# A two-layer attention and state-space trunk: where the norm operations, a table's zeroing, the scaling of u and the layer boundary stand in the order

## The chip, the cores and the metric

The kernel runs on one core of one Trainium2 chip. The metric is the time of one execution on the device in microseconds (us); of several runs the median counts. The engines of the core work side by side, each through its own queue of instructions: TensorE (PE) multiplies, VectorE (DVE) and ScalarE (ACT) do the elementwise work, GpSimd (POOL) and SyncE (SP) are used for a few fills and for issuing DMAs. An instruction that needs another engine's result waits for it at the head of its queue, and everything behind it waits too.

## The reference, cut to what matters

The input is 256 positions of 2048 numbers in float32, and there are two layers. Each layer normalises its input, projects it with one matrix into six parts, runs two branches on them and adds their normalised output projection:

```
h = rmsnorm(x, pre_norm_g[l])
proj = h @ w_in[l]
q, k, v, z_att, u, z_ssm = split(proj)
o_att = diff_attention(q, k, v, lam, rel_bias)
o_att = rmsnorm(o_att, subln_g[l]) * (1.0 - lam_init) * silu(z_att)
y = s5_ssm(u, ...)              # a scan over the positions: 64 groups, 64 complex states
g_val, g_gate = split(gelu(y) @ w_glu[l])
o_ssm = g_val * sigmoid(g_gate) * silu(z_ssm)
mix = concat(o_att, o_ssm) @ w_out[l]
x = x + rmsnorm(mix, post_norm_g[l])
```

## The kernel before

**Weights.** All weights of both layers are streamed once, as 288 half chunks of 512 KB, 144 a layer, in the order u (first four tiles together, "U4", then tiles 4 to 7), q, k, v and z_att, z_ssm ("zs"), glu, out. Each comes by a DMA of SyncE into one of five buffers `raw`. ScalarE copies it to `hi`, a shortened form (fp32r) that TensorE multiplies faster, and VectorE computes `lo` = raw - hi. The activations are split in the same way into `ht` (`hthi` and `htlo`), `mx` or `ghi`/`glo`. TensorE multiplies hi by both halves and lo by the high half, 24 matmuls of 256 columns, or 12 of 512, for a half chunk. hi and lo have three buffers each and are made two half chunks ahead.

**One loop** over the half chunks (line 1224) writes the program. For each it emits the DMA of a later one, `hooks` (which starts generators at given steps s of the layer), `emit_hi` and `emit_lo` of the half chunk two ahead, and `main`, the matmuls. `run_first` and `run_second` advance the generators by one step between those: `prep_gen` (tables `cm`, `z`, `wi`, `gc` of the state-space branch), `rstd_gen` (the norm factor of the layer's input: squares, a chain of norm operations, `psr`, which spreads it over the partitions, and `rbc`, its copy), `s_gen` (`pss`, input of the scan), `scan_ops`, `y_gen` (`psy`, `psz`, gelu, `psg`), attention, and `evac`, which takes the finished sums out of PSUM (`ac` and `acu` are such sums).

**VectorE's fillers.** Two queues hold VectorE work that may go anywhere. `weave` holds long lists (parameters, z, scan), `urgent` holds norm chains: `newton_ops` computes 1/sqrt by two Newton steps (`nwy`, `nwh`; `a` and `scal` are input and result for the attention norm, `nv` and `rs` for one row half at a layer's end, `rst` for a layer's input). Both are emitted by `fill`, half of them before and half behind each lo; the room is `bal`, the planner's estimate of TensorE's time less VectorE's load, with `SPARE` taken off each step and 2880 ns for a step of u, q and k (line 1283). With a norm chain waiting the room is `UB` = 1500 ns, whatever the balance, and norm and weave operations take turns.

**The layer boundary** (lines 1229 to 1265). The last half chunks of the first layer are held back for the second row half, so that row half 0 can be normalised (`rowend(0)`, `add_ops`: `xt`) while TensorE still multiplies for row half 1. Then come one bank of transposes `psw` for the next layer's `wi`, `warm(W3)` dummy matmuls, `rowend(1)`, and `build`, the transposes `psx` of the new `xt` into `ht`. Without ready transposes TensorE can't begin the layer.

**The end.** `rowend(1)`, then `late_mg`: the multiplication of the last 512 columns of `mg` by the norm's weights, on GpSimd; then three pieces of `xt`, each stored by a DMA (TPS).

Of the kernel before, what the change touches and what calls it, by code (L numbers as in the profile page):

```python
# [10 lines left out]
F32 = mybir.dt.float32  # L11
# [28 lines left out]
W3 = 4  # L40
WB = 1
# [7 lines left out]
TPS = ([(0, 1024), (1024, 1024)], [(0, 512), (512, 768), (1280, 768)])  # L49
WY = 2  # L50
UB = 1500
# [35 lines left out]
def hybrid_trunk(ctx: ExitStack, tc, x, rel_bias, post_norm_g, xt_in, wst, vecs, poles, lams, bc, onehot, out):  # L87
# [118 lines left out]
    def fill(budget, force=False):  # L206
        while (budget > 0 and weave) or (urgent and (force or budget > 0)):
            if urgent:
                try:
                    budget -= next(urgent[0])  # L210
                except StopIteration:
                    urgent.popleft()
            if not weave or budget <= 0:
                continue
            try:
                budget -= next(weave[0])
            except StopIteration:
                weave.popleft()
# [19 lines left out]
    def emit_lo(hs, budget, halves=False, parts=(0, 1)):  # L238
        if hs >= 2 * NCH:
            return  # L240
        src, (hi, lo) = raw[hs], split[hs]
        if lo is None:
            lo = late[hs] if hs in late else sp.tile([128, 1024], F32R, tag="lo", name="lo")
        hf = hi.bitcast(F32)
        if (weave and budget > 0) or urgent:
            budget = UB if urgent else budget
            fill(budget / 2)
            tt(lo, src, hf, ALU.subtract)
            fill(budget / 2)
        elif halves:  # L250
            for p in parts:
                c = slice(512 * p, 512 * p + 512)
                tt(lo[:, c], src[:, c], hf[:, c], ALU.subtract)
        else:
            tt(lo, src, hf, ALU.subtract)
        split[hs] = (hi, lo)
        if parts[-1]:
            raw.pop(hs)

    def newton_ops(o, v, n, i=0):  # L260
# [3 lines left out]
        yield ts(y.bitcast(I32), v.bitcast(I32), -0.5, float(0x5F380000), ALU.mult, ALU.add)  # L264
        yield mul(h, y, y)
# [204 lines left out]
    def prep_gen(l, slots):  # L470
# [55 lines left out]
        for b0 in range(0, 8, nb):  # L526
# [11 lines left out]
            for b, ps in zip(range(b0, b0 + nb), pss):  # L538
                psv = ps.rearrange("p (h a g q) -> p h a g q", h=2, a=2, g=2)
                wv = wi[b // 4].rearrange("p (b h r a q) -> p b h r a q", b=4, h=2, r=2, a=2)[:, b % 4]  # L540
                for r in range(2):
                    for g in range(2):
                        act(wv[64 * g:64 * g + 64, :, r], psv[64 * r:64 * r + 64, :, :, g ^ r], AF.Copy)
# [63 lines left out]
    def build(l, m):  # L607
# [7 lines left out]
        for t in range(2):  # L615
            for i in range(2):
                k = 2 * m + i
                tpose(pss[i][:, 256 * i + 128 * t:256 * i + 128 * t + 128], xt[t][:, 128 * k:128 * k + 128], ident)
        for i in range(2):
# [7 lines left out]
    def rstd_gen(l):  # L627
# [43 lines left out]
        if l == 0:  # L671
            yield
# [46 lines left out]
    def s_gen(l):  # L719
# [6 lines left out]
        for b0 in range(0, 8, 2):  # L726
            if b0 == 4:
                while not (S["u2"] and f"wi{l}" in S):
                    yield
                yield  # L730
# [3 lines left out]
            for b in (b0, b0 + 1):  # L734
                wi = S[f"wi{l}" if b >= 4 else f"wa{l}"][b // 4]
                for h in range(2):
                    for a in range(2):
                        for r, g in ((0, 0), (1, 1), (1, 0), (0, 1)):
                            rows, o = slice(64 * g, 64 * g + 64), 64 * (g ^ r)
                            q, c = 2 * h + r, 256 * a + 64 * (2 * (b - b0) + h)  # L740
                            mm4(pss[r][o:o + 64, c:c + 64], wi[rows, b % 4, 2 * q + a], U[rows, 8 * q + b], True, True)
# [208 lines left out]
    def evac(l, seg, b, ac):  # L950
# [6 lines left out]
        if seg in ("U4", "u"):  # L957
            yield from until(f"rbc{l}")
            for j, a in enumerate(ac):
# [3 lines left out]
                mul(o, cut(a[:, 0:256]), cut(rbc))  # L963
        elif seg in ("q", "k"):
# [53 lines left out]
    def main(hs, only=None, part=None):  # L1018
# [3 lines left out]
        if seg == "U4":  # L1022
# [20 lines left out]
            else:  # L1043
                for kk in range(2) if part is None else (part,):
                    for pr in (None,) if part != 0 else range(3):
                        for j in range(4):
                            one(kk, j, pr)
# [79 lines left out]
    def hooks(l, s):  # L1127
# [20 lines left out]
        if s == 96 and l + 1 < DEPTH:  # L1148
# [38 lines left out]
    SPARE = (150.0, 200.0, 300.0)  # L1187
    LOT = 1225.0
    with tc.manual_schedule():
# [34 lines left out]
        for hs in range(2 * NCH):  # L1224
# [4 lines left out]
            if s == 0:  # L1229
# [13 lines left out]
                if l:  # L1243
# [3 lines left out]
                    warm(W3)  # L1247
                    rowend(1)
                    for _ in add_ops(l - 1, 1, [(0, 256), (256, 256)], False):
                        pass  # L1250
# [44 lines left out]
        for t in range(2):  # L1295
# [4 lines left out]
            late_mg(G, (t,))  # L1300
            for _ in add_ops(DEPTH - 1, t, TPS[t], True):
                pass
# [71 lines left out]
```

## Time and profile before

| | us |
|---|---|
| median of 3 runs | 923.97 (923.2 to 924.18) |
| the profiled execution | 924.31 |
| its span, first to last instruction | 922.5 |
| TensorE busy | 901.3 (98%) |
| VectorE busy | 674.2 (73%) |
| ScalarE busy | 487.1 (53%) |
| GpSimd busy | 13.7 (1%) |
| granted TensorE clock, mean | 0.99 |

The rows name an operation as out<-in, with the line of the kernel in front; where a helper emits it, the line is that of the helper (L139 a matmul, L123 a transpose, L142 an elementwise operation of two tensors, L149 one with two operations, L160 an activation). The bracket behind a row is the idle time of the engine just before it, and what ended that. Ends of matmuls are modelled, so durations of neighbours overlap; their starts tell more.

### The profile page before, as it was taken

The page shows a single profiled execution, that of the slowest core. Times are in us where ns is not written, and L with a number is a line of the kernel's source. Part 1 is how long each engine was busy: PE and PEld are TensorE (multiplying, and loading weights), DVE is VectorE, ACT ScalarE, POOL GpSimd, SP SyncE. Part 2 cuts the span into 40 slices and gives each one's busy share as a digit, 9 for nine tenths or more (in the row PEclk, how much of TensorE's full clock was granted, in tenths as well). Part 3 has the DMA queues.
Part 4 walks back from the last instruction along what each step waited for, and adds up shares of the span by engine and source line. Part 5 has one row for each costly group of instructions (what it writes and reads, how often), then busy time and mean ns, then how long its engine had stood idle before and what let it go on. Part 6 is the DMA issues. An engine that isn't in the chain of part 4 may idle for free.

```text
span 922.5 us, 16345 instructions
## 1 busy us (share of the span) xinstructions
PE 901.3 (98%) x6344; PEld 775.3 (84%) x6344; DVE 674.2 (73%) x1202; ACT 487.1 (53%) x878; POOL 13.7 (1%) x19
## 2 busy tenths in 40 slices
PE   9989999999999899999999999999999999999995
PEld 8989999888778688888889888887888888888884
DVE  5978894998975757898677549888966465665564
ACT  6623357465465576444469453445565665644451
POOL 2000000000000000000000000000000000000001
PEclk9999999999999999999999999999999999999998
DMA  8767566755452467567646765865545346665862
GB/s 326 233 190 233 182 218 170 224 176 166 138 183 94 136 224 233 172 226 242 211 152 188 247 209 130 267 198 168 178 137 182 116 138 205 203 208 165 293 181 92
DMA packets 65069, 176.11 MB, mean 191 GB/s; under 512 B 17574, under 2 KB 24512, under 8 KB 64096
## 3 DMA queue, kind: packets, MB, share of 16 engines
q1 hardware_dynamic: 64704, 174.89, 59.9%
q8 instruction: 50, 0.82, 0.4%
q14 instruction: 27, 0.22, 0.1%
q0 software_dynamic: 144, 0.15, 0.1%
q10 hardware_dynamic: 144, 0.03, 0.0%
HBM read 167.42 MB, written 7.88 MB: 190 GB/s over the span
## 4 chain that ended last, share of the span: by engine, by line
PE 86%; DVE 4%; ACT 2%; issue 1%; DVEq 0%; ACTq 0%
PE ac L139 78%; PE lga L139 1%; DVE lo L142 1%; PE psy L139 1%; PE po L139 1%; ACT wi L160 1%; PE pss L139 1%; DVE sct L142 1%; PE acu L139 1%; ACT hi L160 1%; PE pwt L123 1%; PE pst L139 0%; PE psm L123 0%; PE psf L123 0%; DVE nwh L142 0%
## 5 line engine op out<-in xcount | busy, mean ns | idle before, releaser
L160 ACT ACTIVATE hi<-raw 128x1024 fp32r<-128x1024 f32 (+1 forms) x282 | 298.1, 1057 | 358.8 <-PE ac L139 307.7
L142 DVE TENSOR_TENSOR lo<-raw,hi 128x1024 fp32r<-128x1024 f32 (+1 forms) x282 | 343.0, 1218 | 116.5 <-ACT hi L160 113.5
L139 PE MATMUL ac<-ht,hi 128*128 128x256 f32 (+1 forms) x1104 | 257.6, 319 | 3.7 <-DVE u L142 2.5
L139 PE MATMUL ac<-hi,ht 128*128 128x512 f32 x768 | 251.1, 398 | 0.0
L139 PEld LDWEIGHTS ac<-ht,hi 128*128 128x128 f32 x1104 | 184.3, 193 | 18.9 <-issue 2.9
L139 PE MATMUL ac<-ht,lo 128*128 128x256 f32 x704 | 199.3, 284 | 0.4 <-DVE lo L142 0.4
L139 PEld LDWEIGHTS ac<-hi,ht 128*128 128x128 f32 x768 | 144.9, 189 | 31.9
L139 PE MATMUL ac<-lo,ht 128*128 128x512 f32 x384 | 150.8, 393 | 2.1 <-DVE lo L142 2.0
L139 PE MATMUL ac<-hi,mx 128*128 128x512 f32 x456 | 141.8, 390 | 0.0
L139 PEld LDWEIGHTS ac<-ht,lo 128*128 128x128 f32 x704 | 135.2, 192 | 0.9 <-DVE lo L142 0.9
L139 PEld LDWEIGHTS ac<-hi,mx 128*128 128x128 f32 x456 | 85.6, 188 | 17.7
L139 PE MATMUL ac<-lo,mx 128*128 128x512 f32 x228 | 88.7, 389 | 0.0
L139 PEld LDWEIGHTS ac<-lo,ht 128*128 128x128 f32 x384 | 72.6, 189 | 17.5 <-DVE lo L142 3.7
L139 PE MATMUL ac<-hi,ghi 128*128 128x512 f32 x128 | 51.6, 403 | 0.0
L139 PEld LDWEIGHTS ac<-lo,mx 128*128 128x128 f32 x228 | 42.8, 188 | 8.9
L139 PE MATMUL ac<-hi,glo 128*128 128x512 f32 x128 | 50.2, 392 | 0.0
L139 PE MATMUL ac<-lo,ghi 128*128 128x512 f32 x128 | 49.9, 390 | 0.0
L149 DVE SCALAR_TENSOR_TENSOR y<-y 128x512 f32<-128x512 f32 x16 | 11.1, 692 | 28.2 <-ACT y L160 28.0
L160 ACT ACTIVATE att<-att,mx 128x128 f32<-128x128 f32 x64 | 28.4, 446 | 5.4 <-DVE mx L871 5.1
L139 PEld LDWEIGHTS ac<-hi,glo 128*128 128x128 f32 x128 | 24.0, 188 | 5.2
L139 PEld LDWEIGHTS ac<-lo,ghi 128*128 128x128 f32 x128 | 24.1, 188 | 4.6
L139 PEld LDWEIGHTS ac<-hi,ghi 128*128 128x128 f32 x128 | 24.0, 188 | 4.5
(202 smaller groups left out, 964.2 us busy)
## 6 DMA issues: line engine op xcount, KB each, us to landing
raw<-in_wst_dram SPq DMA_DIRECT2D x287, 512.0 KB, 4.0
U<-uds SPq DMA_DIRECT2D x48, 64.0 KB, 3.4
bt<-in_bc_dram SPq DMA_DIRECT2D x4, 512.0 KB, 6.4
uds<-u SPq DMA_DIRECT2D x4, 512.0 KB, 6.0
pg<-in_post_norm_g_dram SPq DMA_DIRECT2D x2, 1024.0 KB, 6.9
xt<-in_x_dram SPq DMA_DIRECT2D x2, 1024.0 KB, 7.4
xt<-xsave SPq DMA_DIRECT2D x2, 1024.0 KB, 6.2
tabs<-tab SPq DMA_DIRECT2D x1, 1536.0 KB, 8.3
```

What stands on the lines that cost most here:

```text
L123: P.transpose(o, i, idn)
L139: P.matmul(o, lhsT=l, rhs=r, start=start, stop=stop, skip_group_check=True)
L142: V.tensor_tensor(o, a, b, op=op)
L149: V.scalar_tensor_tensor(out=o, in0=a, scalar=s, in1=b, op0=op0, op1=op1)
L160: A.activation(out=o, in_=i, func=f, **kw)
```

## The change

Nine edits. (1) `fill` gives norm operations their own 330 ns before each half of the fill and whatever the balance, and weave operations only what the balance allows; UB goes. (2) `newton_ops` for one column (a row half at a layer's end) has seven operations where there were nine. (3) In layer 0 `rstd_gen` emits psr a step earlier, and `evac` of U4 scales its four banks before the three acu. (4) `prep_gen` for the next layer, with its zeroing of cm on GpSimd, its loads bt and its copies, starts at step 102 and not 96, and SPARE for the second part of layer 0 is 100. (5) wi is copied in three pieces a bank and not four. (6) The scan of layer 0 starts one half chunk earlier. (7) At the boundary two banks psw stand ahead of psx, and the dummy matmuls (six, each in two passes) stand behind the first psx. (8) In the first weights the matmuls are ordered hthi, lo, htlo. (9) At the end the multiplication of mg is VectorE's for the second row half, behind the second of three pieces 768, 768, 512.

```diff
-W3 = 4
-WB = 1
+W3 = 0
+WB = 2
+W5 = 6
-TPS = ([(0, 1024), (1024, 1024)], [(0, 512), (512, 768), (1280, 768)])
+TPS = ([(0, 1024), (1024, 1024)], [(0, 768), (768, 768), (1536, 512)])
-UB = 1500
...
-    def fill(budget, force=False):
-        while (budget > 0 and weave) or (urgent and (force or budget > 0)):
-            if urgent:
-                try:
-                    budget -= next(urgent[0])
-                except StopIteration:
-                    urgent.popleft()
-            if not weave or budget <= 0:
-                continue
+    def fill(budget):
+        left = 330.0
+        while urgent and left > 0:
+            try:
+                n = next(urgent[0])
+                left -= n
+                budget -= n
+            except StopIteration:
+                urgent.popleft()
+        while budget > 0 and weave:
...
-            budget = UB if urgent else budget
...
+        if n == 1:
+            w = st.tile([128, n], F32, tag=f"nww{i}", name="nww")
+            yield ts(w, v, 9.0 / 64.0, None, ALU.mult)
+            yield stt(h, y, y, v, ALU.mult, ALU.mult)
+            yield stt(h, h, -10.0 / 3.0, h, ALU.add, ALU.mult)
+            yield stt(y, h, 5.0, y, ALU.add, ALU.mult)
+            yield stt(h, y, y, w, ALU.mult, ALU.mult)
+            yield stt(o, h, -3.0, y, ALU.add, ALU.mult)
+            return
...
-                for r in range(2):
-                    for g in range(2):
-                        act(wv[64 * g:64 * g + 64, :, r], psv[64 * r:64 * r + 64, :, :, g ^ r], AF.Copy)
+                act(wv[:, :, 0], psv[:, :, :, 0], AF.Copy)
+                for g in range(2):
+                    act(wv[64 * g:64 * g + 64, :, 1], psv[64 - 64 * g:128 - 64 * g, :, :, 1], AF.Copy)
...
+            if not m and not t:
+                warm(W5)
...
-        if l == 0:
-            yield
         yield 1
         ps = side("psr")
...
-                yield
+                if l:
+                    yield
...
+            if l == 0 and seg == "u":
+                yield from until("u4")
...
+            if seg == "U4":
+                S["u4"] = True
...
-                for kk in range(2) if part is None else (part,):
-                    for pr in (None,) if part != 0 else range(3):
-                        for j in range(4):
-                            one(kk, j, pr)
+                ks = range(2) if part is None else (part,)
+                if l == 0 and b == 0 or part == 0:
+                    todo = [(kk, pr) for pr in ((0, 2, 1) if part is None else range(3)) for kk in ks]
+                else:
+                    todo = [(kk, None) for kk in ks]
+                for kk, pr in todo:
+                    for j in range(4):
+                        one(kk, j, pr)
...
-        if s == 96 and l + 1 < DEPTH:
+        if s == 102 and l + 1 < DEPTH:
...
-    SPARE = (150.0, 200.0, 300.0)
+    SPARE = (150.0, 100.0, 300.0)
...
-                    warm(W3)
+                    if W3:
+                        warm(W3)
                     rowend(1)
+                    for _ in range(2):
+                        advance(S["prep"])
...
-            late_mg(G, (t,))
-            for _ in add_ops(DEPTH - 1, t, TPS[t], True):
-                pass
+            if not t:
+                late_mg(G, (t,))
+            for n, _ in enumerate(add_ops(DEPTH - 1, t, TPS[t], True)):
+                if t and n == 1:
+                    late_mg(V, (t,))
```

What it moves is seen in the order of the instructions on an engine, at three places.

VectorE where u is scaled, in layer 0 (`pt` is a step of the parameter list, `ac_170` to `ac_173` are U4's four banks), before:

```order
L142 TENSOR_TENSOR lo<-raw,hi 128x1024
L149 SCALAR_TENSOR_TENSOR pt<-pt 128x64 x3
L154 TENSOR_SCALAR pt<-pt 128x64
L142 TENSOR_TENSOR u<-acu,rbc 128x16x4x4 x3
L142 TENSOR_TENSOR u<-ac_170,rbc 128x16x4x4
L142 TENSOR_TENSOR u<-ac_171,rbc 128x16x4x4
L142 TENSOR_TENSOR u<-ac_172,rbc 128x16x4x4
L142 TENSOR_TENSOR u<-ac_173,rbc 128x16x4x4
L142 TENSOR_TENSOR lo<-raw,hi 128x1024
```

and now:

```order
L142 TENSOR_TENSOR lo<-raw,hi 128x1024
L154 TENSOR_SCALAR pt<-pt 128x64
L149 SCALAR_TENSOR_TENSOR pt<-pt 128x64 x3
L142 TENSOR_TENSOR u<-ac_170,rbc 128x16x4x4
L142 TENSOR_TENSOR u<-ac_171,rbc 128x16x4x4
L142 TENSOR_TENSOR u<-ac_172,rbc 128x16x4x4
L142 TENSOR_TENSOR u<-ac_173,rbc 128x16x4x4
L142 TENSOR_TENSOR lo<-raw,hi 128x1024
L142 TENSOR_TENSOR u<-acu,rbc 128x16x4x4 x3
```

The four banks of U4 now stand ahead of lo and of the three acu.

VectorE at the second attention norm chain of layer 0 (`a`, `nwy`, `nwh`, `scal` are the chain; `zs` and `glo` are the gate of the state-space branch and a half of its activations; `y` is gelu's), before:

```order
L154 TENSOR_SCALAR a_3633<-a_3633 128x8
L156 TENSOR_SCALAR nwy<-a_3633 128x8
L142 TENSOR_TENSOR nwh<-nwy 128x8
L142 TENSOR_TENSOR lo<-raw,hi 128x1024
L142 TENSOR_TENSOR nwh<-nwh,a_3633 128x8
L149 SCALAR_TENSOR_TENSOR nwh<-nwh 128x8
L154 TENSOR_SCALAR a_3633<-a_3633 128x8
L149 SCALAR_TENSOR_TENSOR nwy<-nwh,nwy 128x8
L142 TENSOR_TENSOR nwh<-nwy 128x8
L149 SCALAR_TENSOR_TENSOR zs<-th,ac_3208 128x512
L149 SCALAR_TENSOR_TENSOR zs<-th,ac_3209 128x512
L142 TENSOR_TENSOR glo<-psg,ghi 128x16x16 x2
```

and now:

```order
L154 TENSOR_SCALAR a_3625<-a_3625 128x8
L142 TENSOR_TENSOR lo<-raw,hi 128x1024
L156 TENSOR_SCALAR nwy<-a_3625 128x8
L142 TENSOR_TENSOR nwh<-nwy 128x8
L142 TENSOR_TENSOR nwh<-nwh,a_3625 128x8
L149 SCALAR_TENSOR_TENSOR zs<-th,ac_3200 128x512
L149 SCALAR_TENSOR_TENSOR zs<-th,ac_3201 128x512
L142 TENSOR_TENSOR glo<-psg,ghi 128x16x16 x2
L149 SCALAR_TENSOR_TENSOR y<-y 128x512
L149 SCALAR_TENSOR_TENSOR nwh<-nwh 128x8
L154 TENSOR_SCALAR a_3625<-a_3625 128x8
L149 SCALAR_TENSOR_TENSOR nwy<-nwh,nwy 128x8
```

Behind the lo stands the chain's nwy and not its second nwh, and the next operation with one tensor input, `a`, stands behind y and not ahead of zs.

TensorE at the boundary of the layers (`ac_4872` and `ac_4864` are the sum of row half 1, `psw` transposes for wi, `psx` transposes of the new xt), before:

```order
L139 MATMUL ac_4872<-hi,mx 128x512
L123 MATMUL psw<-ident,z_4306 128x128 x4
L139 MATMUL warm<-ones 128x128 x4
L123 MATMUL psx<-ident,xt_4553 128x128 x2
L123 MATMUL psx<-ident,xt_4554 128x128 x2
L123 MATMUL psx<-ident,xt_4553 128x128 x2
L123 MATMUL psx<-ident,xt_4554 128x128 x2
L139 MATMUL ac_5093<-ht,hi 128x256 x2
```

and now:

```order
L139 MATMUL ac_4864<-hi,mx 128x512
L123 MATMUL psw<-ident,z_4298 128x128 x8
L123 MATMUL psx<-ident,xt_4545 128x128 x2
L139 MATMUL warm<-ones 128x128 x6
L123 MATMUL psx<-ident,xt_4546 128x128 x2
L123 MATMUL psx<-ident,xt_4545 128x128 x2
L123 MATMUL psx<-ident,xt_4546 128x128 x2
L139 MATMUL ac_5092<-ht,hi 128x256 x2
```

The dummy matmuls moved behind the first psx, and eight psw stand where four stood.

## Rows read from the trace of the kernel before

**Rows 1.** The page: busy time of each engine, and the granted TensorE clock by slice.

```profile
PE 901.3 (98%) x6344; PEld 775.3 (84%) x6344; DVE 674.2 (73%) x1202; ACT 487.1 (53%) x878; POOL 13.7 (1%) x19
...
PEclk9999999999999999999999999999999999999998
```

**Rows 2.** Waits of TensorE: engine, tile, line <- releaser: us in total, times, longest.

```profile
PE ac L139 <- DVE u L142: 2.5, 1, 2.5
PE ac L139 <- DVE lo L142: 2.4, 4, 0.9
PE psg L123 <- DVE nwh L142: 2.2, 1, 2.2
PE psx L123 <- DVE xt L149: 1.5, 1, 1.5
...
PE ac L139 <- DVE ht L149: 0.9, 1, 0.9
PE pss L139 <- ACT wi L160: 0.3, 1, 0.3
```

**Rows 3.** Stretches: length, busy us (count) by engine, granted clock, DMA share, GB/s.

```profile
50.00:60.00 10.00, 7.49 (x49) 7.12 (x48) 5.98 (x15) 2.39 (x3) 0.00 (x0) 0.83 0.43 139
470.00:480.00 10.00, 9.77 (x66) 9.34 (x67) 6.78 (x15) 7.15 (x17) 0.00 (x0) 0.83 0.55 171
228.00:255.00 27.00, 25.74 (x118) 20.07 (x117) 26.42 (x46) 11.13 (x19) 0.00 (x0) 1.00 0.48 139
```

**Rows 4.** Timeline of TensorE and VectorE at u: start, duration, engine, line, operation, [idle <-releaser].

```profile
50.73 0.59 PE L139 MATMUL psr<-dg,ones 128*128 128x256 f32 x2
53.84 0.47 PE L139 MATMUL ac<-ht,hi 128*128 128x256 f32 x2 [2.51 <-DVE u L142]
...
51.78 1.48 DVE L142 TENSOR_TENSOR u<-acu,rbc 128x256 f32<-128x256 f32 x3 [1.02 <-ACT rbc L160]
53.11 1.98 DVE L142 TENSOR_TENSOR u<-ac,rbc 128x256 f32<-128x256 f32 x4
```

**Rows 5.** Timeline of VectorE at the start of layer 0's scan.

```profile
161.17 1.23 DVE L142 TENSOR_TENSOR sct<-H,a4s 128x1024 f32<-128x1024 f32 x1 [2.02 <-ACT H L160]
```

**Rows 6.** Timeline of VectorE, GpSimd and TensorE at the second norm chain, layer 0.

```profile
306.60 1.22 DVE L142 TENSOR_TENSOR lo<-raw,hi 128x1024 fp32r<-128x1024 f32 x1
...
308.02 1.85 DVE L154 TENSOR_SCALAR a<-a 128x8 f32<-128x8 f32 x1
...
310.01 1.28 DVE L149 SCALAR_TENSOR_TENSOR zs<-th,ac 128x512 f32<-128x512 f32 x2
...
312.19 0.68 DVE L149 SCALAR_TENSOR_TENSOR y<-y 128x512 f32<-128x512 f32 x1
...
313.47 1.22 DVE L142 TENSOR_TENSOR lo<-raw,hi 128x1024 fp32r<-128x1024 f32 x1
...
308.04 1.81 POOL L475 MEMSET cm<- 128x2048 f32 x1 [143.38 <-PE psz L139]
...
313.01 0.63 PE L123 MATMUL psg<-ident,y 128*128 128x128 f32 x4 [2.15 <-DVE nwh L142]
```

**Rows 7.** Timeline of VectorE and GpSimd at the end of the program.

```profile
914.01 1.24 DVE L142 TENSOR_TENSOR nwh<-nwh,nv 128x1 f32<-128x1 f32 x1
...
916.25 2.61 DVE L149 SCALAR_TENSOR_TENSOR xt<-mg,rs,xt 128x512 f32<-128x512 f32 x3
...
913.97 1.26 POOL L1110 TENSOR_TENSOR mg<-mg,pg 128x512 f32<-128x512 f32 x1 [6.87 <-ACT mg L160]
```

**Rows 8.** Timeline of VectorE and TensorE at the boundary of the layers.

```profile
467.80 0.16 DVE L1096 TENSOR_REDUCE nv<-sso 128x1 f32<-128x5 f32 x1 [0.23 <-ACT junk L160]
...
469.54 0.88 DVE L149 SCALAR_TENSOR_TENSOR xt<-mg,rs,xt 128x256 f32<-128x256 f32 x2
...
466.88 0.60 PE L123 MATMUL psw<-ident,z 128*128 128x128 f32 x4
...
470.07 0.88 PE L123 MATMUL psx<-ident,xt 128*128 128x128 f32 x6 [1.48 <-DVE xt L149]
```

More of the change, by code (lines that the diff above doesn't have):

```diff
@@ L740, in s_gen @@
                             q, c = 2 * h + r, 256 * a + 64 * (2 * (b - b0) + h)
-                            mm4(pss[r][o:o + 64, c:c + 64], wi[rows, b % 4, 2 * q + a], U[rows, 8 * q + b], True, True)
+                            mm4(pss[r][o:o + 64, c:c + 64], wi[rows, b % 4, 4 * h + 2 * (r ^ g) + a], U[rows, 8 * q + b], True, True)
             yield
```

## The prediction

> **What bounds the kernel now.** I read first the page's busy shares: TensorE is busy 901.3 of 922.5 us [rows 1], so a change gains only by closing one of TensorE's gaps, by giving back clock that was lost after one, or by a shorter tail behind the last matmul. Then the waits of TensorE [rows 2]: the large ones are one wait for u (2.5), one for the norm operation nwh (2.2), four for lo (2.4), one for xt at the layer boundary (1.5) and one for ht at the start (0.9). Then the clock. The page's line shows full speed in every slice but the last [rows 1], and the finer windows [rows 3] show 10 us with a mean of 0.83 behind the wait for u (50 to 60) and at the boundary (470 to 480); 310 to 320, behind the wait for nwh, is the third such window, with the same 0.83. The clock has two levels, 2.4 and 1.2 GHz, so 0.83 means 10 x 0.17 / 0.5 = 3.4 us at the lower one, in which 1.7 us of work is lost. So these three places cost 2.5 + 1.7, 2.2 + 1.7 and 1.5 + 1.7. The waits for lo, ht and wi, each under 0.9, are followed by no such stretch: 228 to 255 holds two of them at 1.00.
>
> The profiled execution took 924.31 us, its span 922.5; the median of the runs is 923.97. The sum is made against 924.31 and then set 0.34 lower.
>
> **The change part by part.**
>
> *u scaled in order of its banks (layer 0).* Now psr, which spreads the norm factor, stands on TensorE behind the last matmul of u's first seven tiles; it starts at 50.73, VectorE gets to u 1.05 later (51.78), scales three acu first (1.33 to the next operation's start), then the four ac banks, which TensorE waits for to 53.84 [rows 4]. After the change psr stands 24 matmuls earlier, one half chunk, that is 2.88 us by the planner's length of a step (line 1283), and the four ac banks are scaled before lo and before acu. So psr comes at 47.85, the banks are done at 47.85 + 1.05 + 1.98 = 50.9 (the first at 49.4), and TensorE asks for the first at 53.84 - 2.51 = 51.3. The wait goes, and with it the gap that the clock fell after: -2.5 - 1.7 = -4.2. What is late next: lo, which now stands behind the four and ends at 52.1, two steps ahead of its use; that hides it. Ends: -2.5 (clock not regained) and -4.2.
>
> *Start.* Half of the first weights and the second chunk are now multiplied first by hthi, then with lo, then by htlo, so the matmuls that waited 0.9 for the two ht of VectorE stand last. I take -0.8, between -0.3 (lo itself, just before in VectorE's order, is next) and -0.9.
>
> *Three copies of wi for four.* Sixteen ScalarE copies fewer in layer 0; the one wait for wi is 0.3 [rows 2]. -0.25, between 0 and -0.3.
>
> *Scan one half chunk earlier (the yield only in layer 1).* VectorE sat idle for 2.02 before the first sct [rows 5], so the work moves into idle time. But two sct now stand ahead of the next lo and two ahead of the one after: three operations of 1.23 in a step of 2.88, 0.8 too much in each of two steps, 1.6, against the 2.02 that VectorE had idle. Between 0 and +0.8; I take +0.3, near the end that the row speaks for.
>
> *Norm operations with a share of their own.* Before, every lo around 228 to 255 drew two scan operations along with each pair of norm operations: VectorE is busy 26.42 of the 27 us, and TensorE 25.74 [rows 3]: 1.26 idle, two of the four waits for lo [rows 2]. Now an emission gives norm operations 330 ns and the scan only what its balance allows, at most about one scan operation a step. -1.1, between -0.6 and -1.26. The scan then ends when it did (its last operation stands before the same use).
>
> *The second norm chain, 306 to 315.* One a (a TENSOR_SCALAR, 8 elements a partition) took 1.85, beside the memset of cm on GpSimd, 308.04 for 1.81; behind it zs, glo and y slid, y ended at 312.87, TensorE's psg waited 2.2 for it, and the next lo (313.47) cost 0.9 more, one of the four [rows 6]. In the new order the first nwy and nwh stand behind lo 306.60, which therefore starts two norm steps of 0.19 earlier, at 306.2, and ends at 307.4; nwy and two nwh end by 308.0; then come zs, glo and y without a TENSOR_SCALAR among them, and the next a stands behind y, at about 310.7. Zs, glo and y take 312.87 - 310.01 = 2.86, with which they begin at 307.9, so y ends at 310.7, when TensorE gets to psg (313.01 - 2.15 = 310.86). The 2.2 goes; of the lo wait some stays, since the next lo begins only behind y and three norm steps, at 311.1, ends at 312.3, and is needed at 313.47 + 1.22 - 0.9 - 2.15 = 311.65: 0.65 of 0.9. Idle -2.15 - 0.25 = -2.4 (between -1.4 and -2.8), clock -1.7 since a wait of 0.65 is of the size that the clock stood through at 228 to 255 (two in 1.26): -4.1, between -1.4 and -4.5.
>
> *"Next table zeroed later".* The step that emits the memset moves from 96 to 102, but the memset stands first on GpSimd's queue and waits for the last psz that reads its slot, in both kernels. So it still runs at 308.04; this edit alone is worth nothing there. What does move are two loads bt on SyncE's queue (seven weight loads now go ahead of them, the norm row pg stays behind), four copies to cm on ScalarE and the entry of the z operations. They need the tables only at the layer's end, and the weights have five buffers: 0.
>
> Here the Trainium skill says why the form of the operation decides, SBUF — State Buffer, section "Who interferes with whom": the shared port pair is an exclusive lock, a tensor_scalar can take it and is then shut out by any GpSimd operation, while an operation with two SBUF inputs contends only with a GpSimd operation that reads SBUF. The trace agrees: the TENSOR_SCALAR took 1.85 beside a memset, and at the tail nwh, with two inputs, took 1.24 beside GpSimd's multiplication [rows 7]. No sum here needs the rule. By that rule the new order is safe only as long as no TENSOR_SCALAR meets the memset.
>
> *Boundary.* The chain reduce to xt is 469.54 - 467.80 = 1.74 in nine steps, 0.193 each [rows 8]; the new form for one column has seven, so -0.39. One more bank of psw (four transposes, 0.60 by a modelled end; I take 0.4) now fills the wait, and the dummy matmuls, 12 passes in place of 8, stand behind the first psx, where the 1.5 of idle were. Idle falls to about 0.4; by the same reading as above the clock stays up, -1.7, the least sure of the three since the gap is filled with small matmuls. The three copies of wi stand ahead of ht on ScalarE but end before psx does. -0.4 - 0.4 - 1.7 = -2.5, between -0.8 and -2.5.
>
> *Layer 1: psr one step later.* One lo now stands between; rbc still comes about 1.8 before the banks are needed: 0.
>
> *Tail.* GpSimd's multiplication, 1.26, held VectorE's nwh for 1.24 instead of 0.16 [rows 7]. Now VectorE does it, behind two pieces of xt: -1.1 of stall, -0.39 for the shorter chain, +0.65 for the multiplication (512 of the 2048 columns that three xt do in 2.61). The pieces are 768, 768, 512, so the last store is 256 KB and not 384 KB, which no row here prices; I take -0.2, between 0 and -0.4. -1.05, between -0.6 and -1.4.
>
> Sum: -0.8 - 4.2 - 0.25 + 0.3 - 1.1 - 4.1 - 2.5 - 1.05 = -13.7, and 0.2 back for small waits of lo at the end of layer 0, where SPARE now lets prep work go earlier: -13.5. 924.31 - 13.5 - 0.34 = 910.5. With every part at its good end (0.9 + 4.2 + 0.3 + 0 + 1.26 + 4.5 + 2.5 + 1.4 = 15.1) it is 908.9.
>
> **The rivals.**
> *One clock loss stays*, at the boundary or at 313, because what is left idle there is enough: +1.7, 912.2. For: the boundary is filled with 128-column work. Against: full clock behind every wait under 0.9.
> *The memset still meets a TENSOR_SCALAR.* nwy, a TENSOR_SCALAR too, has to be through before 308.04; by the sum it begins at 307.4. If lo slides by over 0.6, nwy is held for 1.8 as a was [rows 6], zs, glo and y slide as before, and nearly all of the 4.1 comes back: 914.4. Nothing in the order keeps the two apart but time.
> *A new wait for every gap closed*: rbc in layer 1 late (2.5 + 1.7), and lo behind two sct (0.8 and a clock loss of 1.7), or two of the rivals together: 914 to 919.
> *Nothing lands*: the waits are TensorE's only in name, another engine sets the pace: 923.5. Against: TensorE is busy 98% of the time [rows 1].
> *Slower*: the clock falls inside a stretch that now has no gap. Place: 57 to 470, where the waits for u, lo and nwh had broken TensorE's work. Price: each us at 1.2 GHz loses 0.5. It decides from 28 us at the lower level on, which eat the 13.7; with 35 it ends at 927.8. Against: TensorE worked 25.74 of 27 us at 1.00 in 228 to 255 [rows 3], and all slices but the last show the full clock [rows 1].
>
> **How the numbers follow.** Forecast, 908.9 to 911.5: 0.52. One clock loss, 911.5 to 913.3: 0.15. Memset, 913.3 to 915.6: 0.13. Several new waits, 915.6 to 922: 0.09. More than the good ends: 0.05. Nothing: 0.03. Slower: 0.03. The first three hold 0.80, so the range goes from 908.5 to 916.0. A measurement of this kernel tells about 0.2% (1.85 us) from no change; by that bound faster has 0.94, same 0.03, slower 0.03.
>
> **What would show it.** Right: no wait for u and no low clock at 50 to 60; no wait over 0.6 at psg and the lo behind it, and no TENSOR_SCALAR over 0.3 beside the memset, still at the same place relative to psz; clock 1.00 at 470 to 480; nwh of 0.16 at the tail and xt begun 1.35 behind the reduce. Wrong: a low clock at one of the three places without a wait over 0.6 before it, or a new wait for lo at the first sct or for u in layer 1.

## The result, and the profile after

The changed kernel took 910.8 us (median of 4 runs, 909.46 to 911.21), the kernel before 923.76 (4 runs, 923.2 to 924.18): ratio 0.9858, 95% interval 0.984 to 0.9875. The forecast was 910.5. The profiled execution of the changed kernel took 909.46, its span 907.7, so by the two traces the gain is 14.85 and by the medians 13.0; the difference is taken up further down.

The page (busy share, and the clock by slice) and TensorE's waits, as in [rows 1] and [rows 2]:

```profile
PE 895.6 (99%) x6348; PEld 771.7 (85%) x6348; DVE 669.6 (74%) x1195; ACT 480.5 (53%) x862; POOL 12.5 (1%) x18
...
PEclk9999999999999999999999999999999999999998
```

```profile
...
PE ac L139 <- DVE lo L142: 0.8, 2, 0.5
PE ac L139 <- ACT ht L160: 0.3, 1, 0.3
PE psx L123 <- DVE xt L149: 0.3, 1, 0.3
```

The waits for u and nwh are gone from the list, that for xt fell from 1.5 to 0.3, and lo from four waits with 2.4 to two with 0.8. The windows that answer to [rows 3] (columns as there; everything stands up to 14 us earlier now):

```profile
50.00:60.00 10.00, 10.00 (x86) 10.00 (x85) 9.26 (x26) 4.10 (x4) 0.00 (x0) 1.00 0.67 211
300.00:310.00 10.00, 9.54 (x46) 7.09 (x42) 9.49 (x22) 5.20 (x11) 1.81 (x1) 1.00 0.51 154
...
460.00:470.00 10.00, 10.00 (x88) 10.00 (x87) 8.81 (x18) 8.14 (x19) 0.00 (x0) 1.00 0.59 193
228.00:255.00 27.00, 27.00 (x127) 21.77 (x126) 24.81 (x53) 14.44 (x27) 0.00 (x0) 1.00 0.63 191
```

All three low stretches are gone (310 to 320 reads 1.00 too). 228 to 255 has TensorE busy for the whole 27 us.

At u, where [rows 4] had the wait of 2.51 (timeline, TensorE and VectorE):

```profile
47.06 0.59 PE L139 MATMUL psr<-dg,ones 128*128 128x256 f32 x2
...
48.11 2.08 DVE L142 TENSOR_TENSOR u<-ac,rbc 128x256 f32<-128x256 f32 x4 [1.02 <-ACT rbc L160]
50.02 1.22 DVE L142 TENSOR_TENSOR lo<-raw,hi 128x1024 fp32r<-128x1024 f32 x1
51.16 1.58 DVE L142 TENSOR_TENSOR u<-acu,rbc 128x256 f32<-128x256 f32 x3
```

psr starts at 47.06 and VectorE gets to u 1.05 later, as before; but it takes the four banks first, and TensorE, which asks for them at 50.4, does not wait.

At the second norm chain ([rows 6]; VectorE, GpSimd, TensorE):

```profile
299.46 0.17 DVE L156 TENSOR_SCALAR nwy<-a 128x8 int32<-128x8 int32 x1
...
302.17 0.68 DVE L149 SCALAR_TENSOR_TENSOR y<-y 128x512 f32<-128x512 f32 x1
...
300.18 1.81 POOL L485 MEMSET cm<- 128x2048 f32 x1 [135.83 <-PE psz L139]
...
303.00 0.63 PE L123 MATMUL psg<-ident,y 128*128 128x128 f32 x4
...
304.32 0.50 PE L139 MATMUL ac<-lo,ht 128*128 128x512 f32 x1 [0.46 <-DVE lo L142]
```

The memset runs at the same place, 2.93 behind the y ahead of the chain (308.04 - 305.10 in the trace before is 2.94). But nwy ends at 299.63, 0.55 ahead of it, and nothing beside it is a TENSOR_SCALAR. y ends at 302.85, psg starts at 303.00 without a wait, and of the lo behind it 0.46 is left (the prediction had 0.65).

At the boundary ([rows 8]; TensorE):

```profile
455.28 1.03 PE L123 MATMUL psw<-ident,z 128*128 128x128 f32 x8
456.15 0.38 PE L123 MATMUL psx<-ident,xt 128*128 128x128 f32 x2
456.37 1.50 PE L139 MATMUL warm<-ones 128*128 128x128 f32 x12
458.21 0.88 PE L123 MATMUL psx<-ident,xt 128*128 128x128 f32 x6 [0.34 <-DVE xt L149]
```

and at the end ([rows 7]; VectorE):

```profile
899.46 0.16 DVE L1117 TENSOR_REDUCE nv<-sso 128x1 f32<-128x5 f32 x1 [3.07 <-ACT junk L160]
...
900.93 1.95 DVE L149 SCALAR_TENSOR_TENSOR xt<-mg,rs,xt 128x768 f32<-128x768 f32 x2
902.80 0.68 DVE L1131 TENSOR_TENSOR mg<-mg,pg 128x512 f32<-128x512 f32 x1
903.52 0.75 DVE L149 SCALAR_TENSOR_TENSOR xt<-mg,rs,xt 128x512 f32<-128x512 f32 x1
```

The chain from reduce to xt takes 900.93 - 899.46 = 1.47 (the prediction had 1.35; its two steps with three inputs take 0.25 and not 0.19), where before it took 1.74 at the boundary and 2.81 here (reduce at 913.44, xt at 916.25), with GpSimd beside it.

The same matmuls can be found in both traces, and how much earlier each starts says where the gain came from:

| TensorE reaches | before | after | gained so far | this part |
|---|---|---|---|---|
| psu (behind the start and u) | 130.85 | 125.83 | 5.02 | 5.0: start 0.75, u 4.27 |
| lga, first (behind wi and the scan's start) | 176.57 | 170.90 | 5.67 | 0.65 |
| lga, fifth (behind the first norm chain) | 252.65 | 244.84 | 7.81 | 2.1 |
| psf (behind the second norm chain) | 335.64 | 324.04 | 11.60 | 3.8 |
| pss of layer 1 (behind the boundary) | 527.76 | 513.77 | 13.99 | 2.4 |
| po, last but one (most of layer 1) | 744.55 | 730.57 | 13.98 | 0.0 |
| end of the span | 922.5 | 907.7 | 14.8 | 0.8 |

### The profile page after: what moved, and what is told of

It reads as the page before. It is cut to its first block, busy times and chain, and to the rows that moved or that the text cites. A ratio compares the mean times of both kernels' runs of the same rounds, so it can differ in the third digit from the quotient of the medians.

```text
span 907.7 us, 16326 instructions
## 1 busy us (share of the span) xinstructions
PE 895.6 (99%) x6348; PEld 771.7 (85%) x6348; DVE 669.6 (74%) x1195; ACT 480.5 (53%) x862; POOL 12.5 (1%) x18
## 4 chain that ended last, share of the span: by engine, by line
PE 93%; DVE 3%; ACT 1%; DMA 1%; issue 1%; SPq 0%; ACTq 0%; DVEq 0%
PE ac L139 83%; PE acu L139 3%; PE lga L139 1%; PE po L139 1%; PE psy L139 1%; PE pss L139 1%; DVE lo L142 1%; DMA raw<-in_wst_dram 1%; PE psw L123 1%; PE pwt L123 1%; PE pst L139 0%; DVE sct L142 0%; PE psf L123 0%; PE psm L123 0%; DVE xt L149 0%
## 5 line engine op out<-in xcount | busy, mean ns | idle before, releaser
L139 PE MATMUL ac<-ht,hi 128*128 128x256 f32 (+1 forms) x1104 | 253.2, 316 | 0.6 <-ACT ht L160 0.3
L139 PE MATMUL ac<-ht,lo 128*128 128x256 f32 x704 | 196.3, 282 | 0.4 <-DVE lo L142 0.4
L139 PEld LDWEIGHTS ac<-ht,hi 128*128 128x128 f32 x1104 | 181.1, 191 | 15.4 <-ACT ht L160 0.8
L139 PEld LDWEIGHTS ac<-ht,lo 128*128 128x128 f32 x704 | 133.1, 190 | 0.7 <-DVE lo L142 0.7
```

The costliest lines, as they stand in the source:

```text
L139: P.matmul(o, lhsT=l, rhs=r, start=start, stop=stop, skip_group_check=True)
```

## The experiments

Twelve kernels. Those whose names begin with a are the kernel before with one thing changed, the others the changed kernel with something undone or added. Times are medians of 4 to 10 runs; the kernel before had 923.85 (19 runs), 923.56 (7) and 924.05 (7) beside them. The changed kernel was not run again beside them, so a difference of under about 1 us from its 910.8 says little by itself; such differences are read from the traces.

### a1: the share of the norm operations alone

The diff is that of `fill` and of UB shown above, and nothing else.

> The kernel before with the first edit alone: norm operations get 330 ns of their own in each half of a fill, UB goes; the table is still zeroed from step 96 on. Theory: this edit mends two places by itself, because it changes which operation stands beside the memset of cm and thins the scan operations between lo: the waits for lo around 246 to 250 go (2.1 us by the two traces) and the wait of psg at 313 with its low clock goes (3.7 us by the two traces), so about 918 us. Rival, the words of the change: the second place is mended by zeroing the table later, so this edit alone brings 2.1 and ends at 921.7, with a TENSOR_SCALAR of over 1 us beside the memset.

Measured: 915.98, ratio 0.9929 (0.9905 to 0.9954), so 7.9 less, 60% of the whole gain by one edit, and more than either theory had. Clock windows, GpSimd and VectorE:

```profile
310.00:320.00 10.00, 10.00 (x136) 8.15 (x135) 5.63 (x8) 6.96 (x17) 1.81 (x1) 1.00 0.47 148
460.00:470.00 10.00, 8.36 (x64) 7.51 (x63) 7.59 (x25) 6.29 (x15) 0.00 (x0) 1.00 0.28 87
...
314.25 1.81 POOL L475 MEMSET cm<- 128x2048 f32 x1 [149.35 <-PE psz L139]
...
314.27 0.68 DVE L149 SCALAR_TENSOR_TENSOR y<-y 128x512 f32<-128x512 f32 x1
```

By its trace the kernel is 8.5 faster: 2.0 up to the fifth lga, 4.15 more up to psf, 2.1 more up to the first pss of layer 1 (the boundary) and 0.2 behind it. Wait and low clock at 310 to 320 are gone though the table is still zeroed from step 96 on. They went in a way that I had not worked out: the scan's last operation ends at 276.5 and not at 252.4, so the last psz and with it the memset come 6.2 later, at 314.25, when the norm chain is long through; beside it stand glo, y and lo, which it doesn't hold. So the prediction's "the scan then ends when it did" does not hold for this edit by itself. And the clock stands at 460 to 470 although the wait for xt is as long as it was (1.49): the trace gains 1.5 there.

### a2: the later table alone

```diff
-        if s == 96 and l + 1 < DEPTH:
+        if s == 102 and l + 1 < DEPTH:
```

> The kernel before with the table's generator started at step 102 and not 96, and nothing else. Theory: the memset waits on GpSimd for the same psz and runs at the same 308.0, the TENSOR_SCALAR a still takes about 1.85 beside it, psg still waits 2.2, so no change: 923.5 to 924.2. Rival, the words of the change: the memset runs later, the wait goes, 3.7 us less, 920.2.

Measured: 923.64, ratio 1.0001 (0.9988 to 1.0015). VectorE, GpSimd and the clock in one window:

```profile
307.86 1.86 DVE L154 TENSOR_SCALAR a<-a 128x8 f32<-128x8 f32 x1
...
307.89 1.81 POOL L475 MEMSET cm<- 128x2048 f32 x1 [142.50 <-PE psz L139]
...
310.00:320.00 10.00, 6.99 (x22) 5.09 (x21) 9.09 (x16) 4.09 (x10) 0.00 (x0) 0.68 0.39 127
```

The memset starts at 307.89 and a is held for 1.86 as before. The line was moved in the program and the memset stayed, since GpSimd had nothing else to do and waited for another engine's result. The last row is the clock: psg waited 2.15 as before, but 0.68 means 10 x 0.32 / 0.5 = 6.4 us at the lower level, where the kernel before had 3.4 behind the same wait.

### a3: the same place, another form

```diff
-        yield ts(v, v, 9.0 / 64.0, None, ALU.mult)
+        yield stt(v, v, 9.0 / 64.0, ones[:, 0:n], ALU.mult, ALU.mult)
```

> The kernel before with one operation in another form: the a that scales by 9/64 in the norm chain takes a second tensor of ones and two operations (SCALAR_TENSOR_TENSOR) in place of a TENSOR_SCALAR; it stands in the same place, does the same arithmetic and runs beside the same memset. Theory: the form decides, so this a takes 0.2 beside the memset, y ends 1.7 earlier, the wait of psg falls from 2.15 to about 0.4; lo behind it still waits about 1. 1.7 us less if the clock is lost all the same, 3.3 if not: 920.5 to 922. Rival: any operation of VectorE is held by the memset, then it takes 1.85 again and nothing changes.

Measured: 920.17, ratio 0.9965 (0.9951 to 0.9978), 3.7 less, slightly under the range given; by its trace it is 3.0 ahead at psf (332.61 against 335.64). VectorE, GpSimd and the clock in one window:

```profile
308.02 0.16 DVE L149 SCALAR_TENSOR_TENSOR a<-a,ones 128x8 f32<-128x8 f32 x1
...
308.05 1.81 POOL L475 MEMSET cm<- 128x2048 f32 x1 [143.27 <-PE psz L139]
...
310.00:320.00 10.00, 8.56 (x41) 6.62 (x40) 8.82 (x15) 6.11 (x12) 0.00 (x0) 1.00 0.47 142
```

Same place, same memset, 0.03 apart: 0.16 where it took 1.85. The form decides, as the Trainium skill has it (SBUF — State Buffer, "Who interferes with whom"): a tensor_scalar can be shut out by any GpSimd operation, one with two SBUF inputs not by a memset, which only writes. The same section lets the order of issue decide which of two such operations waits; the two starts lie 0.02 to 0.03 apart here, and starts on GpSimd are rough, so this can't be read from these traces. psg waited 0.6 and lo 0.9 here, and the clock stood through both.

### b7: the memset meets a TENSOR_SCALAR in the changed kernel

```diff
             tt(lo, src, hf, ALU.subtract)
+            if hs == 90:
+                tt(lo[:, 0:768], src[:, 0:768], hf[:, 0:768], ALU.subtract)
             fill(budget / 2)
```

> The changed kernel with one operation more: three quarters of one lo are computed twice (0.85 us of VectorE), just ahead of the nwy of the second norm chain, so that this TENSOR_SCALAR falls inside the memset. Theory, the rival of the prediction that the memset meets a TENSOR_SCALAR: nwy is held until the memset ends, about 1.6, y slides by 0.85 + 1.6, psg waits about 2.3 and the clock falls behind it: 4 us more than the changed kernel, about 914.5. Other theory: nwy is not held, then psg waits 0.7 and the whole is 0.9 longer, 911.7, at full clock.

Measured: 913.48 (911.44 to 913.94), ratio 0.9894 (0.9872 to 0.9917), 2.7 more than the changed kernel. VectorE, GpSimd, and the clock in two windows:

```profile
300.50 1.55 DVE L156 TENSOR_SCALAR nwy<-a 128x8 int32<-128x8 int32 x1
...
300.22 1.81 POOL L487 MEMSET cm<- 128x2048 f32 x1 [135.22 <-PE psz L139]
...
300.00:310.00 10.00, 7.48 (x34) 5.42 (x27) 9.43 (x21) 4.31 (x10) 1.81 (x1) 0.87 0.35 107
310.00:320.00 10.00, 10.00 (x45) 8.20 (x45) 6.97 (x9) 4.34 (x6) 0.00 (x0) 0.96 0.58 170
```

nwy was held to the end of the memset (1.55), psg waited 2.0 and started 2.37 later than in the changed kernel, and the clock fell: 3.7 by the trace, of which some 0.9 would by the other theory be the added operation's own. The one run of the four at a mean clock of 0.998 took 911.44, the three at 0.994 and 0.995 took 913.1 to 913.9, so perhaps the clock did not fall in that one. So this rival was real, at a price somewhat under the 4.1 of the prediction, and the changed kernel stays clear of it by 0.55 us and by nothing else.

### b2 and b3: either half of the edit on u

b2 puts the yield ahead of psr back, b3 the order of the banks:

```diff
         yield from until(f"rst{l}")
+        if l == 0:
+            yield
         yield 1
...
-            if l == 0 and seg == "u":
-                yield from until("u4")
+            if l == 0 and seg == "U4":
+                yield from until("u6")
...
-            if seg == "U4":
-                S["u4"] = True
+            if b == 6:
+                S["u6"] = True
```

> The changed kernel with psr of layer 0 one half chunk later again (the yield put back), the banks of U4 still scaled first. Theory: the order of the banks alone takes most of the wait, because the first bank is then done 1.05 + 0.5 behind psr: psr at 49.95, first bank at 51.5, TensorE asks at about 50.7, a wait of about 0.8 that the clock stands through: about 1 us more than the changed kernel, 911.8. Rival: psr's place is the part that counts, then the wait is 2.5 again with a low clock, 4.2 more, 915.

> The changed kernel with the three acu scaled ahead of the four banks of U4 again, psr still a step earlier. The third acu is finished by TensorE only at about 50.3, so the first bank is done at about 51.3. Theory: a wait of about 0.9 at full clock, 1.1 more than the changed kernel, 911.9: either edit alone does most of the work. Rival: the order of the banks is the part that counts, 2.5 and the clock come back, 915.

Measured: b2 911.68, ratio 0.9871 (0.9851 to 0.9892); b3 911.37, ratio 0.9867 (0.9849 to 0.9885). TensorE's waits for u, of b2:

```profile
PE ac L139 <- DVE u L142: 1.1, 1, 1.1
```

and of b3:

```profile
PE ac L139 <- DVE u L142: 1.4, 1, 1.4
```

Each half alone brings the wait from 2.5 to 1.1 or 1.4, at full clock in the profiled executions, and costs 0.6 to 0.9 against having both by the medians, whose intervals overlap, and 1.36 (b2) and 1.06 (b3) by the traces (psu at 127.19 and 126.89 against 125.83). So the two overlap: most of the 4.2 is there with either.

### b1 and b8: the filling of the boundary

b1 leaves out the dummy matmuls (W5 = 0). b8 fills as before (W3 = 4, W5 = 0, WB = 1, without the two extra steps of the generator); the short chain stays in both.

> The changed kernel without its six dummy matmuls (12 passes) at the boundary of the layers. They feed nothing, so psx should start as before, with some 1.8 us idle in front of it in place of 0.34. Theory: the filler earns its place by the clock alone; without it the clock falls behind the gap as it did behind the 1.48 of the kernel before, about 1.5 us more, 912.3. Rival: the clock came back because the gap got shorter by the chain and by psw, and the filler brings nothing: 910.8.

> The changed kernel with the boundary filled as before: one bank of psw, four dummy matmuls (eight passes) ahead of the first psx, none behind it; the shorter norm chain stays. Theory: only the bank of psw that moved into the wait is worth anything, 0.4 by its row, since without the dummy matmuls the clock stood; the wait of psx is about 1.1: 0.4 more than the changed kernel, 911.2. Rival, the prediction's term: the filling also keeps the clock, which now falls in most executions, 1.5 more on top, 912.7, with a mean clock of 0.995 or less in most.

Measured: b1 910.47 (909.76 to 911.3), ratio 0.9858 (0.984 to 0.9875); b8 909.38 (909.24 to 909.62), ratio 0.9847 (0.9832 to 0.9861). TensorE at the boundary and the clock around it, of b1:

```profile
458.06 0.87 PE L123 MATMUL psx<-ident,xt 128*128 128x128 f32 x6 [1.68 <-DVE xt L149]
...
455.00:460.00 5.00, 3.17 (x23) 2.40 (x22) 3.58 (x13) 3.78 (x11) 0.00 (x0) 1.00 0.28 105
460.00:465.00 5.00, 5.00 (x44) 5.00 (x44) 3.95 (x8) 4.01 (x8) 0.00 (x0) 1.00 0.45 129
```

and of b8:

```profile
458.44 0.88 PE L123 MATMUL psx<-ident,xt 128*128 128x128 f32 x6 [1.22 <-DVE xt L149]
```

TensorE waits 1.68 and 1.22, and the clock stands in both traces up to the last matmuls; the runs of b8 have mean clocks of 0.996 to 0.998. The filling brings nothing that can be measured in the whole, neither the dummy matmuls nor the bank of psw that moved: by the traces b8 is 0.24 behind at the first pss of layer 1 and 0.04 behind at psu, 16 us later, and 0.18 of it stood there before the boundary (fifth lga at 245.02 against 244.84). The theory's 0.4 for psw is there at first: from the six psx to psr b8 takes 32.86, the changed kernel 32.43. But from psr to the first pss it takes 22.71 and not 23.13, at full clock and without a wait in either: the same matmuls follow each other more closely, and why is not known. Whether b8 is better than the changed kernel the two intervals don't tell.

### b4: the scan's start

> The changed kernel with the scan of layer 0 started one half chunk later again (the yield put back). The prediction put +0.3 on the earlier start. Theory by the two traces, in which no wait for lo appears there: worth nothing either way, within 0.3 of the changed kernel, 910.8. Rival: the 0.6 that the change won between 142 and 148 came from it and not from the copies of wi: 911.4, with the loss at that place.

The edit takes `if l:` away from the yield in `s_gen`. Measured: 909.63 (909.37 to 910.67), ratio 0.985 (0.9833 to 0.9867). In the trace pss of the third pair comes 2.8 later and lga behind it at the same time within 0.1. An earlier scan is worth nothing and costs nothing; the 0.65 of that stretch is by elimination that of the copies of wi, which were not tried alone (a1, with the edit of `fill`, takes 45.70 from psu to the first lga, the kernel before 45.72, the changed kernel 45.07).

### b5: the end

```diff
-            if not t:
-                late_mg(G, (t,))
+            late_mg(G, (t,))
```

> The changed kernel with the last multiplication of mg on GpSimd again, ahead of the three pieces of xt; the pieces stay 768, 768, 512 and the chain short. Theory: one norm operation of the chain is held for about 1.1 beside it, and VectorE is spared the 0.65 of the multiplication, so the last piece of xt ends about 0.4 later than in the changed kernel. Rival: nothing in the new chain is held, then it ends 0.65 earlier.

Measured: 910.91, ratio 0.9863 (0.9848 to 0.9878): no difference in the medians. VectorE:

```profile
900.18 1.18 DVE L149 SCALAR_TENSOR_TENSOR nwh<-nwh 128x1 f32<-128x1 f32 x1
...
902.03 2.61 DVE L149 SCALAR_TENSOR_TENSOR xt<-mg,rs,xt 128x768 f32<-128x768 f32 x3
```

One operation of the chain, now the second nwh, is held for 1.18; the last xt ends at 904.64, against 904.27 in the changed kernel, whose matmuls end 0.09 earlier. The span ends 0.7 later (908.5 against 907.7, less 0.09), perhaps because the three stores also stand closer together. It is as large as expected or somewhat larger, and too small for the medians.

### b6: the start

The edit puts the loop over hthi, htlo, lo back for every bank.

> The changed kernel with the matmuls of the first weights in the order of before (hthi, htlo, lo for each bank). Theory: the wait for ht comes back at 11.4, 0.9 by its row and 0.8 by the two traces, and nothing after it gives that back: 0.8 more, 911.6. Rival: the loads of the weights set the pace of the first 50 us (they run at full share there) and the 0.8 is given back by the first scaling of u: 910.8.

Measured: 911.38, ratio 0.9869 (0.9853 to 0.9886). TensorE waits 0.9 for ht again, psr starts 0.83 later than in the changed kernel, and it is not given back anywhere. The rival's premise holds from 10 to 20 only (DMA share 1.02 there in the changed kernel, then 0.88, 0.60 and 0.73).

### A version meant to be better

```diff
-    def fill(budget):
-        left = 330.0
+    def fill(budget, left=0.0):
...
             tt(lo, src, hf, ALU.subtract)
-            fill(budget / 2)
+            fill(budget / 2, 660.0)
...
-[(0, 768), (768, 768), (1536, 512)]
+[(0, 768), (768, 768), (1536, 256), (1792, 256)]
```

> The changed kernel with two edits more: norm operations only behind a lo, with 660 ns in place of 330 ahead and 330 behind, and the last piece of xt cut in two of 256 columns, so that the last store is 128 KB. Theory: the wait of 0.46 for lo at 304 goes, with what its row hides some 0.6, and the last store lands 0.25 earlier: 0.8 less than the changed kernel, 910.0. Rival: three norm operations and two of four columns more stand in front of something else, the nwy of the second chain meets the memset, and it is 2 to 3 slower.

Measured: 912.28 (911.33 to 912.9), ratio 0.9877 (0.9862 to 0.9892), 1.5 slower than the changed kernel. TensorE's waits:

```profile
PE ac L139 <- DVE u L142: 2.2, 2, 1.1
```

The 0.46 at 304 fell to 0.19, and the last store landed 0.2 earlier behind the last xt. But the norm chain of the layer's input lost its places ahead of lo in both layers, psr came 2.1 and 3.4 later, and TensorE waited 1.1 for u twice. At psu the kernel is 0.6 behind the changed kernel in layer 0 and 1.9 in layer 1. The loss came by the wait that the edit on u had closed in layer 0 and by a new one in layer 1, not by the memset that the rival named.

## Why the prediction was right, and where its terms were off

| part | predicted | by the traces | by an experiment |
|---|---|---|---|
| start | -0.8 | -0.75 | -0.83 (b6, trace) |
| u | -4.2 | -4.27 | either half alone: 0.6 to 0.9 short of it |
| wi and scan's start | +0.05 | -0.65 | scan's start 0 (b4) |
| first norm chain | -1.1 | -2.1 | with the next: -6.2 (a1, trace up to psf) |
| second norm chain | -4.1 | -3.8 | -3.0 by trace, -3.7 by medians (a3, another remedy) |
| later table | 0 | | 0 (a2) |
| boundary | -2.5 | -2.4, of it the clock 1.5 | filling: 0 (b1, b8) |
| end | -1.05 | -0.8 | -0.7 (b5, trace) |

*Right by its own steps:* the start, u, the second norm chain, the later table that moves nothing, the end. The hidden cover that each rests on was there: lo behind the four banks was not waited for, nwy cleared the memset by the half microsecond that was given.

*The step on the first norm chain was too small by 1.0.* It took TensorE's loss from its idle time, 1.26 in 228 to 255, and that understates it. TensorE's timeline of the kernel before, where lo came late several times in a row:

```profile
242.02 0.61 PE L139 MATMUL ac<-hi,ht 128*128 128x512 f32 x2
242.77 0.50 PE L139 MATMUL ac<-lo,ht 128*128 128x512 f32 x1
...
245.17 0.61 PE L139 MATMUL ac<-hi,ht 128*128 128x512 f32 x2
246.37 0.50 PE L139 MATMUL ac<-lo,ht 128*128 128x512 f32 x1 [0.59 <-DVE lo L142]
```

Two hi matmuls and then lo: undisturbed, lo starts 0.46 behind the pair. Here it starts 0.75 behind it at 242.02, 0.29 too late, and no idle time is shown, since the modelled end of the last hi covers half of that; and 1.20 behind it at 245.17, 0.74 too late, of which 0.59 is shown. Behind each wait the next matmul also starts about 0.11 later than usual (lo 0.50 long and not 0.39). So each wait cost some 0.25 more than its bracket, and the small one showed none. The same stretch of matmuls (from po at 230.65 to lga at 252.65) is 22.00 long before and 19.85 after.

*The wi term was too small as well:* it too took the bracket of the wait, 0.3, for the whole loss, and the stretch gained 0.65; how much of that a hidden wait is, is not shown. The scan's +0.3 was not there (b4).

*The clock term of the boundary, -1.7, was not the change's to gain.* The step that failed is "by the same reading as above the clock stays up": I took one execution's low clock for a property of the place. The kernel before, a1, a2 and a3 all waited 1.48 or 1.49 for xt; the clock fell in the first only. TensorE of a2, and its clock behind the wait:

```profile
471.21 0.87 PE L123 MATMUL psx<-ident,xt 128*128 128x128 f32 x6 [1.48 <-DVE xt L149]
...
470.00:480.00 10.00, 8.64 (x69) 8.20 (x70) 8.10 (x20) 7.48 (x18) 0.00 (x0) 1.00 0.53 168
```

From the six psx to the first pss of layer 1 TensorE takes 57.69 before, 56.23 in a2, 56.22 in a3 and 55.56 in the changed kernel, and ahead of those psx the change gains 0.26. So of the 2.4 that the traces show at the boundary, about 0.9 came with the change, near the -0.4 - 0.4 for chain and psw, and 1.5 is the clock, which stood in a2 and a3 with the old boundary too. Nor did it fall behind 1.68 in b1, 1.22 in b8, 1.37 in b3. In 19 runs of the kernel before, the mean clock goes from 0.990 (three runs, 924.0 to 926.7 us) over 0.992 and 0.993 (most) to 0.995 (920.35), while the changed kernel's runs have 0.997 or 0.998. So behind the waits of 2.5 and 2.15 for u and nwh, and of 1.95 in b7, the clock fell in the traces that I have, and behind those of 1.2 to 1.7 in some executions at most. The Trainium skill (TensorE: Matmul & The Clock Gate, "Part 1: The HAM clock gate") states that the chip's activity window runs free and doesn't start over with the kernel, so that one kernel meets it at different points in different runs; it says this of a kernel's start, and that it holds for gaps in the middle is my inference. The traces agree as far as they go: equal waits, different clocks. What chance a wait of 1.5 has, these few traces do not tell.

*Nor is 1.7 a fixed price.* From psg to psf TensorE takes 21.17 in a3, where the clock stood, 22.63 in the kernel before and 23.91 in a2: behind equal waits of 2.15 the fall cost 1.5 in one execution and 2.7 in the other.

So the sum of 13.5 was met by 13.0 with errors of opposite sign in it: about 1.0 too little for waits that TensorE's brackets hide, 0.7 too little for wi and the scan, and up to 1.7 too much for a clock that falls only sometimes. That they nearly cancel is luck. The 14.85 of the two traces is more than the 13.0 of the medians because of the executions that were profiled: that of the kernel before lies 0.55 above its median, that of the changed kernel, the fastest of its four, 1.34 below.

*The words of the change* were right in the place and wrong in the reason: norm operations with a share of their own are the main part, but in the changed kernel the second place was mended because the norm chain moved, not because the table was zeroed later.

## What to carry to other kernels

Before moving work to another time, look what its queue waits for: the memset here, alone on its engine, ran when its buffer was free, wherever the program emitted it (a2). Where a small operation takes ten times its usual time, look at what GpSimd does beside it, and at the operation's form before its place. Cost a wait of TensorE by the distance between the starts of the same matmuls in a quiet and in a disturbed step, not by the idle time shown; and don't count a low clock behind a wait of 1 to 2 us as surely gained until a second execution shows it. Before a difference of about 1 us between two traces is put down to an edit, look whether the same matmuls, without a wait between them, took the same time in both.

## What the runs showed of the hardware

- A memset on GpSimd held a one-input TENSOR_SCALAR of 8 elements for 1.85, 1.86 and 1.55 (to the memset's end), and a SCALAR_TENSOR_TENSOR with two SBUF inputs at the same place not at all (0.16).
- A multiplication on GpSimd, with two inputs, held an operation of VectorE with two SBUF inputs: 1.24 before, 1.18 in b5, against 0.16.
- Equal waits of TensorE of 1.48 to 1.49 were followed by 1.2 GHz in one of four traces; equal waits of 2.15 in both traces that have one, for 3.4 us in one and for more than 6 in the other.
- Weights can come late in one execution and not in the next. ScalarE and TensorE at the start of b1, then ScalarE in the changed kernel:

```profile
7.60 0.63 ACT L160 ACTIVATE hi<-raw 128x512 fp32r<-128x512 f32 x1 [1.73 <-DMA raw<-in_wst_dram]
8.28 1.22 PE L139 MATMUL ac<-ht,hi 128*128 128x256 f32 x8 [0.85 <-ACT hi L160]
...
7.14 0.63 ACT L160 ACTIVATE hi<-raw 128x512 fp32r<-128x512 f32 x1 [0.20 <-DMA raw<-in_wst_dram]
```

TensorE's wait of 0.9 for hi in b1 cost nothing in the end: at the first pss b1 is 0.1 ahead (137.49 against 137.60).

- The same matmuls can take longer at the same clock. Layer 1 from the last pss to the first lga, in b1 and in the changed kernel:

```profile
537.63:618.32 80.69, 80.32 (x498) 68.75 (x497) 70.56 (x129) 34.37 (x45) 0.00 (x0) 1.00 0.66 196
...
537.78:617.36 79.58, 79.21 (x498) 68.65 (x497) 70.23 (x129) 34.28 (x45) 0.00 (x0) 1.00 0.66 200
```

Either has the same 498 matmuls and one wait of 0.37; b1 takes 1.1 longer, more than the 0.9 by which its span is longer. What sets the distance between the matmuls no run here shows. It is also of the size by which runs of the changed kernel differ at equal mean clocks (909.46 to 911.21).
